# A two-layer hybrid decoder on one core: block 0's gate matmuls after the third input projection, output weights loaded later, the last products on VectorE

## The chip, the cores and the metric

The kernel runs on one core of one Trainium2 chip. The metric is the device time of one execution in microseconds; the time before is the median of three runs, 927.42 us (927.25 to 930.23). The engines are TensorE (PE in the profile), VectorE (DVE), ScalarE (ACT), GpSimd (POOL), and SyncE (SP), which here issues nearly all DMAs.

## What is computed

Input x is 1024 x 1024 in float32. Layer 0 mixes tokens by latent attention with 12 heads, layer 1 by a gated linear recurrence over 12 x 64 channels; both also attend with 4 heads to 256 memory tokens. In each layer:

```python
z = h @ w_in                                   # mixer inputs | gate | memory queries
tok = causal_attention(...) or rg_lru_branch(u, ...)
mem_out = memory_attention(q_mem, mem_k, mem_v)
y = concatenate([tok, mem_out], -1) * silu(gate)
h = layer_norm(ALPHA * h + y @ w_out[layer], ln_g[layer], ln_b[layer])
# the recurrence of layer 1:
xc = conv_b + sum(u_pad[:, tap:tap + s] * conv_w[tap] for tap in range(4))
r, i = sigmoid(xc @ w_r + b_r), sigmoid(xc @ w_i + b_i)      # per block of 64
a = exp(-8 * softplus(-lam) * r)
hs = scan(a, sqrt(1 - a * a) * (i * xc))
```

## The kernel before

Every product is made of three matmuls (`mm3`, lines 110 to 115): each operand is split into a high half in fp32r and a low half, the rest; hi*hi, hi*lo and lo*hi are added up in PSUM. `split` (86 to 90) makes the halves: ACT, DVE or POOL copies the high one (line 82 on POOL, 84 on ACT), and DVE always subtracts to get the low one (line 90). `load_w` (99) brings a weight into one of two staging tiles `wf` and splits it into a ring of two hi/lo tiles; a staging tile is free for the next load when its split is done.

The Tile framework builds one list of instructions per engine from the program's order and its own estimates; an engine runs its list in order and waits at a row until its semaphores are there.

*Layer 0.* `main_head` gives the attention of a head as units: scores, two exponentials (558, 559), a subtraction for the low half of the probabilities (561, mostly POOL), and the products with the values (569). `run_units` (592) runs a head pair's 28 units, and between them takes steps of the generators in `fills`: `n` steps over the units. For the last pair, p = 5 (line 812), the fill is the memory's load, keys and values, the row maxima of two memory heads, and four steps of `wgen`, which loads and splits the eight 128-row pieces of the output weights (`load_wout`, 775). Then the memory attention runs in two pairs of heads (817 to 823), whose fills take one, one and two steps of `wgen`; line 825 takes whatever steps are left.

When the second head of a pair is through, `finish_pair` (621) divides by the softmax sums: two DMAs bring the sums `den` to `rn`, DVE inverts them (625), two DMAs write them to `den_d`, two more broadcast them into `Of` (630), and POOL multiplies (631). Slots 0 to 5 are the head pairs of layer 0, slots 6 and 7 its two memory pairs, slots 8 and 9 those of layer 1. Slot 7's product is on `GA[3]`, printed GA_75.

The output projection `out_proj` (831) starts with a group of three row tiles s = 0, 1, 2: first the feature pieces k = 0 to 3 of all three, then k = 4 to 7. `ymm0` (923) loads the rows of y from `y_d` into `Pf` (929) and splits them into R16 and R17 in turn (printed R_70 and R_71; lines 84 and 934); piece 7 comes from GA[3] itself.

*Layer 1.* Six blocks of 128 channels: `lru_u` is the input projection (48 matmuls), `lru_copy` (995) copies it out of PSUM by ACT, `lru_conv` (999) is the convolution, one instruction of line 1002 and three of 1005 on DVE, with a split, and `lru_rest` (1009) holds the 12 gate matmuls with XH and XL, the activations and the scan. The two first projections come ahead of the list. The string `ORD` (1062) sets the program order of all the rest: c copy, v convolution, r gates and scan, u projection, q memory query projection, g gate projections of the memory part. U, XC, XH, XL, RR and II have two buffers each, one for even and one for odd blocks. Behind it, `pd` opens over the freed buffers and loads the keys, values and queries of the memory attention (1089 on).

Of the kernel before, what the change touches and what calls it, by code (L numbers as in the profile page):

```python
# [15 lines left out]
ALU = mybir.AluOpType  # L16
# [28 lines left out]
def hybrid_kernel(ctx: ExitStack, tc: tile.TileContext, io):  # L45
    nc = tc.nc
    PE, ACT, DVE, POOL, SP = nc.tensor, nc.scalar, nc.vector, nc.gpsimd, nc.sync
# [25 lines left out]
    R = [pr[1].tile([128, S], F32R, name=f"R{i}") for i in range(12)]  # L73
# [3 lines left out]
    def f32(ap):  # L77
        return ap.bitcast(F32)
# [18 lines left out]
    def wsplit(src, hi, lo):  # L97
        split(src, hi, lo, weng[0])

    def load_w(ap, n):  # L100
        j = wjob[0]
        wjob[0] += 1
        st = wf[j % 2][:, :n]
        SP.dma_start(st, ap)
        nb = len(ring["hi"])
        hi, lo = ring["hi"][j % nb], ring["lo"][j % nb]
        wsplit(st, hi[:, :n], lo[:, :n])
        return hi, lo

    def mm3(out, parts):  # L110
        n = len(parts)
        for i, (lh, ll, rh, rl) in enumerate(parts):
            PE.matmul(out, lh, rh, start=(i == 0), stop=False)  # L113
            PE.matmul(out, lh, rl, start=False, stop=False)  # L114
            PE.matmul(out, ll, rh, start=False, stop=(i == n - 1))  # L115
# [59 lines left out]
    with tc.manual_schedule(engines={mybir.EngineType.DVE}):  # L175
# [20 lines left out]
        for k in range(3, 8):  # L196
# [4 lines left out]
                       fill=1.0, base=0, channel_multiplier=1)  # L201
    POOL.memset(cmask, 0.0)
    POOL.affine_select(out=cmask[:, 384:512], in_=cmask[:, 384:512], pattern=[[-1, 128]], compare_op=ALU.is_ge,
                       fill=-1e30, base=0, channel_multiplier=1)
    POOL.memset(cmaskT, 0.0)
    POOL.affine_select(out=cmaskT, in_=cmaskT, pattern=[[1, 128]], compare_op=ALU.is_ge,
                       fill=-1e30, base=0, channel_multiplier=-1)
# [183 lines left out]
    def rope_rows(h):  # L391
        r0 = (h % 4) * 32
        SP.dma_start(f32(sets[h % 4][2])[64:96, :], qr_d[h // 4, 0, r0:r0 + 32, :])
        SP.dma_start(f32(sets[h % 4][3])[64:96, :], qr_d[h // 4, 1, r0:r0 + 32, :])
# [15 lines left out]
    def next_m():  # L410
        mi[0] += 1
        return mbank[mi[0] % len(mbank)]
# [11 lines left out]
    def neg_max_row(mx, dst_row):  # L424
        nm = small.tile([128, 8], F32, tag="nm", name="nm")
        DVE.tensor_reduce(out=nm, in_=mx, axis=AX.X, op=ALU.max, negate=True)

        def row():
            ps = next_m()
            PE.transpose(ps[0:8, 0:128], nm, ident)  # L430
            nmt = small.tile([8, 128], F32R, tag="nmt", name="nmt", bufs=1)
            DVE.tensor_copy(nmt, ps[0:8, 0:128])
            SP.dma_start(f32(dst_row()).rearrange("o (a b) -> o a b", a=8), f32(nmt))
        rows.append([DELAY, row])
# [31 lines left out]
    r1 = slice(32, 64)  # L466
# [119 lines left out]
    def chain(*gens):  # L586
        for g in gens:
            yield from g
# [32 lines left out]
    def finish_pair(gt, slot):  # L621
        rn = small.tile([128, 16], F32, tag="rn", name="rn")
        for e in range(2):
            SP.dma_start(rn[:, e * 8:(e + 1) * 8], den[32 * e:32 * e + 1, :].rearrange("o (a b) -> o a b", a=128))
        DVE.reciprocal(rn, rn)
        for e in range(2):
            SP.dma_start(den_d[slot, e].rearrange("(a b) -> a b", a=128), rn[:, e * 8:(e + 1) * 8])
        rec = Of[slot % 2]
        for e in range(2):
            SP.dma_start(rec[e * 64:(e + 1) * 64, :], den_d[slot, e:e + 1, :].broadcast_to([64, S]))  # L630
        POOL.tensor_tensor(out=gt, in0=gt, in1=rec, op=ALU.mult)

    SC = 1.0 / math.sqrt(96.0)

# [48 lines left out]
    def mem_load():  # L683
        for i in range(2):
            j = wjob[0]
            wjob[0] += 1
            SP.dma_start(wf[j % 2], io["memT"][i])
            wsplit(wf[j % 2], R[i], R[2 + i])
        yield

    def mem_kv(layer):
        KH, KL = (R[4], R[5]) if layer == 0 else (R[8], R[9])
        VmH, VmL = (R[6], R[7]) if layer == 0 else (R[0], R[1])
        pk = next_m()
        for m in range(2):
            hi, lo = load_w(io["wmk"][layer, m], S)
            out = pk[:, m * 256:(m + 1) * 256]
            mm3(out, [(hi[:, k * 128:(k + 1) * 128], lo[:, k * 128:(k + 1) * 128], mTh[k], mTl[k]) for k in range(8)])
            yield
        for e in range(2):  # L700
            src = pk[e * 64:(e + 1) * 64, 0:512].rearrange("p (m k) -> p m k", m=2)
            oh = KH[0:64, :].rearrange("p (m e k) -> p m e k", m=2, e=2)[:, :, e, :]
            ol = KL[0:64, :].rearrange("p (m e k) -> p m e k", m=2, e=2)[:, :, e, :]
            o2 = KH[64:128, :].rearrange("p (m e k) -> p m e k", m=2, e=2)[:, :, e, :]
            ACT.copy(oh, src)
            ACT.copy(o2, src)
            DVE.tensor_tensor(out=ol, in0=src, in1=f32(oh), op=ALU.subtract)
        POOL.memset(f32(KL)[64:65, :], 1.0)
        wv = [load_w(io["wmv"][layer, i], S) for i in range(2)]
        pv_ = next_m()  # L710
        for kt in range(2):
            parts = []
            for k in range(8):
                hi, lo = wv[k // 4]
                c = slice((k % 4) * 256, (k % 4 + 1) * 256)
                parts.append((mTh[k][:, kt * 128:(kt + 1) * 128], mTl[k][:, kt * 128:(kt + 1) * 128], hi[:, c], lo[:, c]))
            mm3(pv_[:, kt * 256:(kt + 1) * 256], parts)
            yield
        src = pv_.rearrange("p (t h d) -> p t h d", t=2, h=4)
        oh = VmH[:, 0:520].rearrange("p (t h d) -> p t h d", t=2, h=4)  # L720
        ol = VmL[:, 0:520].rearrange("p (t h d) -> p t h d", t=2, h=4)
        ACT.copy(oh[:, :, :, 0:64], src)
        DVE.tensor_tensor(out=ol[:, :, :, 0:64], in0=src, in1=f32(oh)[:, :, :, 0:64], op=ALU.subtract)
        POOL.memset(f32(oh)[:, :, :, 64:65], 1.0)
        POOL.memset(f32(ol)[:, :, :, 64:65], 0.0)
        if layer == 1:
            SP.dma_start(mem_d[0], f32(KH))
            SP.dma_start(mem_d[1, 0:65], f32(KL)[0:65, :])
            SP.dma_start(mem_d[2, :, 0:520], f32(VmH)[:, 0:520])
            SP.dma_start(mem_d[3, :, 0:520], f32(VmL)[:, 0:520])  # L730

    def mem_max(layer, m, q1, q2, KH):
        r0 = (m % 2) * 64
        SP.dma_start(f32(q1)[0:64, :], qmem_d[layer][m // 2, 0, r0:r0 + 64, :])
        SP.dma_start(f32(q1)[64:128, :], qmem_d[layer][m // 2, 1, r0:r0 + 64, :])
        SP.dma_start(f32(q2)[0:64, :], qmem_d[layer][m // 2, 0, r0:r0 + 64, :])
        mx = small.tile([128, 8, 2], F32, tag="mx", name="mx")
        POOL.memset(mx, -3.0e38)
        for i4 in range(4):
            ps = next_m()  # L740
            for i2 in range(2):
                i = i4 * 2 + i2
                PE.matmul(ps[:, i2 * 256:(i2 + 1) * 256],
                          q1[:, i * 128:(i + 1) * 128], KH[:, m * 256:(m + 1) * 256], start=True, stop=True)
            DVE.tensor_reduce(out=mx[:, i4 * 2:i4 * 2 + 2, 0:1], in_=ps.rearrange("p (a b) -> p a b", a=2),
                              axis=AX.X, op=ALU.max)
            yield
        neg_max_row(mx, lambda: q2[64:65, :])
        yield
# [36 lines left out]
    MQ = [sets[m][2:4] for m in range(4)]  # L786
# [4 lines left out]
    wgen = load_wout(0, wt, woh, wol)  # L791

    def take(g, n):
        for _ in range(n):
            next(g, None)
            yield

    for p in range(6):
        units = main_head(2 * p) + main_head(2 * p + 1)
        fill, n = [], 0  # L800
        if p < 5:
            rope_rows(2 * p + 2)
            rope_rows(2 * p + 3)
            fill.append(qk_proj(p + 1))
            n += 4
            if p % 2 == 1:
                fill.append(v_proj((p + 1) // 2))
                n += 4
            fill += [max_pass(2 * p + 2), max_pass(2 * p + 3)]
            n += 28  # L810
        else:
            fill += [mem_load(), mem_kv(0), mem_max(0, 0, *MQ[0], R[4]), mem_max(0, 1, *MQ[1], R[4]), take(wgen, 4)]
            n = 19
        fills = [(chain(*fill), n, 0, len(units))]
        run_units(units, fills)
    mbank[:] = [bank[6], bank[7]]
    for q in range(2):
        units = mem0(2 * q) + mem0(2 * q + 1)
        if q == 0:
            fill, n = chain(mem_max(0, 2, *MQ[2], R[4]), take(wgen, 1), mem_max(0, 3, *MQ[3], R[4]), take(wgen, 1)), 12  # L820
        else:
            fill, n = chain(mem_kv(1), take(wgen, 2)), 6
# [236 lines left out]
                DVE.tensor_tensor(out=G1[m][:, cs], in0=ps[n], in1=G1[m][:, cs], op=ALU.mult)  # L1059
            yield  # L1060

    ORD = 'c0 v0 c1 v1 r0 u2 c2 v2 r1 u3 c3 v3 r2 u4 c4 v4 r3 u5 c5 v5 r4 q0 r5 q1 g6 g7'
    for it in ORD.split():
        t = int(it[1])
        if it[0] == 'c':
# [135 lines left out]
```

## Time and profile before

| | |
|---|---|
| median of 3 runs | 927.42 us (927.25 to 930.23) |
| profiled execution | 928.3 us, span 926.5 us |
| mean granted clock of TensorE | 0.993 of full |
| busy: PE, DVE, ACT, POOL | 897.6, 607.4, 438.1, 224.6 us |
| DMA | 96.09 MB, mean 104 GB/s |

The span is the time between the first and the last instruction that the profile shows; 1.8 us of the execution lie around it. Busy times of the engines overlap. An idle time in brackets stands in front of an instruction and names what ended it. Of TensorE's clock, 1.00 is 2.4 GHz and 0.50 is 1.2 GHz.

### The profile page before, as it was taken

The page shows a single profiled execution, that of the slowest core. Times are in us where ns is not written, and L with a number is a line of the kernel's source. Part 1 is how long each engine was busy: PE and PEld are TensorE (multiplying, and loading weights), DVE is VectorE, ACT ScalarE, POOL GpSimd, SP SyncE. Part 2 cuts the span into 40 slices and gives each one's busy share as a digit, 9 for nine tenths or more (in the row PEclk, how much of TensorE's full clock was granted, in tenths as well). Part 3 has the DMA queues.
Part 4 walks back from the last instruction along what each step waited for, and adds up shares of the span by engine and source line. Part 5 has one row for each costly group of instructions (what it writes and reads, how often), then busy time and mean ns, then how long its engine had stood idle before and what let it go on. Part 6 is the DMA issues. An engine that isn't in the chain of part 4 may idle for free.

```text
span 926.5 us, 12547 instructions
## 1 busy us (share of the span) xinstructions
PE 897.6 (97%) x4477; PEld 733.6 (79%) x4477; DVE 607.4 (66%) x1309; ACT 438.1 (47%) x747; POOL 224.6 (24%) x219
## 2 busy tenths in 40 slices
PE   9999999999999999999999999988999999999996
PEld 8998788877787778779677878866888877678886
DVE  7953256258777768795784498746998154457865
ACT  4423211217676677777785122117997156753000
POOL 5101033011536354473771200000000022210000
PEclk9999999999999999999999999998999999999999
DMA  9102134324022213155657552111112911252311
GB/s 329 44 23 100 54 111 147 96 76 106 15 58 69 59 58 104 33 160 142 196 144 230 175 180 102 68 69 46 46 46 104 242 54 47 69 181 93 137 72 65
DMA packets 45658, 96.09 MB, mean 104 GB/s; under 512 B 10874, under 2 KB 19866, under 8 KB 45596
## 3 DMA queue, kind: packets, MB, share of 16 engines
q1 hardware_dynamic: 45164, 94.60, 32.6%
q8 instruction: 35, 0.57, 0.3%
q10 hardware_dynamic: 432, 0.69, 0.2%
q14 instruction: 27, 0.22, 0.1%
HBM read 71.94 MB, written 23.16 MB: 103 GB/s over the span
## 4 chain that ended last, share of the span: by engine, by line
PE 79%; DVE 7%; ACT 4%; issue 3%; DMA 3%; POOL 2%; SPq 0%; DVEq 0%; ACTq 0%; POOLq 0%
PE bank L113 10%; PE bank L114 10%; PE bank L115 10%; PE bank L569 7%; PE bank L654 5%; PE bank L844 5%; PE bank L843 5%; PE bank L842 5%; PE bank L364 3%; PE bank L366 3%; PE bank L365 3%; PE bank L154 2%; PE bank L155 2%; PE bank L153 2%; PE bank L451 2%
## 5 line engine op out<-in xcount | busy, mean ns | idle before, releaser
L561 POOL TENSOR_TENSOR pl<-Pf,ph 128x512 fp32r<-128x512 f32 (+1 forms) x99 | 125.4, 1277 | 116.5 <-ACT ph L559 102.8
L558 ACT ACTIVATE Pf<-bank 128x512 f32<-128x512 f32 (+1 forms) x152 | 86.5, 569 | 52.6 <-DVE bank L555 20.8
L654 PE MATMUL bank<-st,st 96*128 96x512 f32 (+7 forms) x432 | 106.0, 344 | 0.1
L90 DVE TENSOR_TENSOR R<-wf,R 128x1024 fp32r<-128x1024 f32 (+4 forms) x43 | 52.1, 1214 | 64.2 <-POOL R L82 60.1
L654 PEld LDWEIGHTS bank<-st,st 96*128 96x128 f32 (+1 forms) x432 | 76.0, 190 | 13.3 <-ACT ph L559 0.6
L559 ACT ACTIVATE ph<-bank 128x512 fp32r<-128x512 f32 (+1 forms) x136 | 76.4, 563 | 0.1
L82 POOL TENSOR_SCALAR R<-wf 128x1024 fp32r<-128x1024 f32 (+3 forms) x25 | 24.1, 966 | 197.1 <-PE bank L114 95.6
L113 PE MATMUL bank<-R,R 128*128 128x256 f32 (+1 forms) x190 | 63.2, 333 | 0.7 <-ACT Pf L372 0.4
L114 PE MATMUL bank<-R,R 128*128 128x256 f32 (+1 forms) x190 | 62.3, 328 | 0.0
L115 PE MATMUL bank<-R,R 128*128 128x256 f32 (+1 forms) x190 | 62.2, 327 | 0.0
L453 DVE CUSTOM_DVE_ANT_0 bank<-bank,cmask 128x384 f32<-128x384 f32 (+4 forms) x96 | 48.8, 518 | 10.7 <-PE bank L451 9.8
L364 PE MATMUL bank<-xh,R 128*128 128x512 f32 x128 | 50.8, 397 | 0.1
L366 PE MATMUL bank<-xh,R 128*128 128x512 f32 x128 | 50.7, 396 | 0.0
L365 PE MATMUL bank<-xl,R 128*128 128x512 f32 x128 | 50.5, 395 | 0.0
L569 PE MATMUL bank<-ph,VH 128*65 128x512 f32 (+2 forms) x144 | 49.5, 344 | 0.0
L569 PE MATMUL bank<-pl,VH 128*65 128x512 f32 (+2 forms) x144 | 45.3, 341 | 2.4 <-POOL pl L561 2.0
L569 PE MATMUL bank<-ph,VL 128*65 128x512 f32 (+2 forms) x144 | 47.1, 338 | 0.0
L843 PE MATMUL bank<-wo,yh 128*128 128x512 f32 (+1 forms) x126 | 47.0, 373 | 0.0
L842 PE MATMUL bank<-wo,yh 128*128 128x512 f32 (+1 forms) x126 | 46.6, 370 | 0.0
L844 PE MATMUL bank<-wo,yl 128*128 128x512 f32 (+1 forms) x126 | 45.9, 368 | 0.0
L114 PE MATMUL bank<-HTl,rg 128*128 128x512 f32 x112 | 44.4, 396 | 0.0
L113 PE MATMUL bank<-HTh,rg 128*128 128x512 f32 x112 | 44.3, 396 | 0.0
(314 smaller groups left out, 2390.5 us busy)
## 6 DMA issues: line engine op xcount, KB each, us to landing
wf<-w SPq DMA_DIRECT2D x26, 512.0 KB, 3.6
wf<-wout SPq DMA_DIRECT2D x16, 512.0 KB, 3.9
Of<-den_d SPq DMA_DIRECT2D x20, 256.0 KB, 3.6
GA<-x SPq DMA_DIRECT2D x8, 512.0 KB
h_d<-GA SPq DMA_DIRECT2D x8, 512.0 KB, 2.6
GA<-h_d SPq DMA_DIRECT2D x8, 512.0 KB, 4.1
y_d<-GA SPq DMA_DIRECT2D x7, 512.0 KB
out<-GA SPq DMA_DIRECT2D x7, 512.0 KB
```

Source lines behind the costliest of these rows:

```text
L113: PE.matmul(out, lh, rh, start=(i == 0), stop=False)
L114: PE.matmul(out, lh, rl, start=False, stop=False)
L115: PE.matmul(out, ll, rh, start=False, stop=(i == n - 1))
L364: PE.matmul(ps[n], hi[:, ks], xh[k][:, cs], start=(k == 0), stop=False)
L366: PE.matmul(ps[n], lo[:, ks], xh[k][:, cs], start=False, stop=(k == 7))
L558: ACT.activation(pf[:, :n], ps[:, :n], AF.Exp, scale=scale)
L561: lo_eng.tensor_tensor(out=lo[:, :n], in0=pf[:, :n], in1=f32(hi)[:, :n], op=ALU.subtract)
L569: mm.append(lambda: PE.matmul(ops[0:65, q0:q0 + w], st, mv[:, c0:c0 + w], start=start, stop=stop))
L654: yield lambda: PE.matmul(ps[:, c0:c0 + w], k[0:r, ks], q[0:r, qs], start=(i == 0), stop=(i == 2))
L842: PE.matmul(out, hi, woh[k][:, ns], start=(k == ko[0]), stop=False)
L843: PE.matmul(out, hi, wol[k][:, ns], start=False, stop=False)
L844: PE.matmul(out, lo, woh[k][:, ns], start=False, stop=(k == ko[7]))
```

## The change

Three edits. `finish_pair` multiplies on DVE instead of POOL for slots 7, 8 and 9. The fill of the last head pair loses its four steps of `wgen`, and n goes from 19 to 15; the later takes of one, one and two and line 825 stay as they are. `ORD` is written anew: each block's gates r follow the projection of two blocks later, which itself moves ahead of the next convolution; r4 and r5 follow q0 and q1.

```diff
@@ -628,7 +628,8 @@
-        POOL.tensor_tensor(out=gt, in0=gt, in1=rec, op=ALU.mult)
+        eng = DVE if slot >= 7 else POOL
+        eng.tensor_tensor(out=gt, in0=gt, in1=rec, op=ALU.mult)
@@ -809,8 +810,8 @@
-            fill += [mem_load(), mem_kv(0), mem_max(0, 0, *MQ[0], R[4]), mem_max(0, 1, *MQ[1], R[4]), take(wgen, 4)]
-            n = 19
+            fill += [mem_load(), mem_kv(0), mem_max(0, 0, *MQ[0], R[4]), mem_max(0, 1, *MQ[1], R[4])]
+            n = 15
@@ -1059,7 +1060,7 @@
-    ORD = 'c0 v0 c1 v1 r0 u2 c2 v2 r1 u3 c3 v3 r2 u4 c4 v4 r3 u5 c5 v5 r4 q0 r5 q1 g6 g7'
+    ORD = 'c0 v0 c1 u2 v1 r0 c2 v2 u3 c3 r1 v3 u4 c4 r2 v4 u5 c5 r3 v5 q0 r4 q1 r5 g6 g7'
```

From line 632 on, a line of the changed kernel has a number higher by one. How the lists of the engines change is shown at two places.

VectorE at the first convolutions of layer 1, before. XC_5437, XH_5439 and XL_5441 belong to block 0, XC_5438 and XL_5442 to block 1; R_71 is the low half of the third projection's weights, rg_5431 that of the fourth's:

```order
L1002 TENSOR_SCALAR XC_5437<-U_5435,vecs 128x1024
L1002 TENSOR_SCALAR XC_5438<-U_5436,vecs 128x1024
L1005 SCALAR_TENSOR_TENSOR XC_5437<-U_5435,vecs,XC_5437 128x1024
L1005 SCALAR_TENSOR_TENSOR XC_5438<-U_5436,vecs,XC_5438 128x1024
L1005 SCALAR_TENSOR_TENSOR XC_5437<-U_5435,vecs,XC_5437 128x1024
L1005 SCALAR_TENSOR_TENSOR XC_5438<-U_5436,vecs,XC_5438 128x1024
L1005 SCALAR_TENSOR_TENSOR XC_5437<-U_5435,vecs,XC_5437 128x1024
L1005 SCALAR_TENSOR_TENSOR XC_5438<-U_5436,vecs,XC_5438 128x1024
L90 TENSOR_TENSOR XL_5441<-XC_5437,XH_5439 128x1024
L90 TENSOR_TENSOR R_71<-wf_82,R_70 128x1024
```

and of the change:

```order
L1003 TENSOR_SCALAR XC_5437<-U_5435,vecs 128x1024
L1003 TENSOR_SCALAR XC_5438<-U_5436,vecs 128x1024
L1006 SCALAR_TENSOR_TENSOR XC_5437<-U_5435,vecs,XC_5437 128x1024
L1006 SCALAR_TENSOR_TENSOR XC_5438<-U_5436,vecs,XC_5438 128x1024
L1006 SCALAR_TENSOR_TENSOR XC_5437<-U_5435,vecs,XC_5437 128x1024
L90 TENSOR_TENSOR R_71<-wf_82,R_70 128x1024
L1006 SCALAR_TENSOR_TENSOR XC_5437<-U_5435,vecs,XC_5437 128x1024
L1006 SCALAR_TENSOR_TENSOR XC_5438<-U_5436,vecs,XC_5438 128x1024
L90 TENSOR_TENSOR XL_5441<-XC_5437,XH_5439 128x1024
```

R_71 moved up, ahead of three convolution steps; the second row, the first step of block 1, stands where it stood. On TensorE the 12 gate matmuls of block 0 moved from ahead of the third projection's first product with R_71 to behind the projection's last.

VectorE at the start of layer 0's output projection, before. R_70<-Pf_76, R_71<-Pf_77 and R_70<-Pf_78 are the low halves of y for row tiles 0, 1 and 2, pieces 0 to 3:

```order
L618 TENSOR_TENSOR GA_75<-bank_87,GA_75 64x512
L561 TENSOR_TENSOR pl_114<-Pf_79,ph_110 128x512
L934 TENSOR_TENSOR R_70<-Pf_76,R_70 128x512
L618 TENSOR_TENSOR GA_75<-bank_88,GA_75 64x512
L934 TENSOR_TENSOR R_71<-Pf_77,R_71 128x512
L625 RECIPROCAL rn<-rn 128x16
L934 TENSOR_TENSOR R_70<-Pf_78,R_70 128x512
```

and of the change:

```order
L935 TENSOR_TENSOR R_70<-Pf_76,R_70 128x512
L618 TENSOR_TENSOR GA_75<-bank_87,GA_75 64x512
L561 TENSOR_TENSOR pl_114<-Pf_79,ph_110 128x512
L90 TENSOR_TENSOR st_1_1782<-wf_82,st_0_1781 128x1024
L618 TENSOR_TENSOR GA_75<-bank_88,GA_75 64x512
L90 TENSOR_TENSOR st_1_1786<-wf_83,st_0_1785 128x1024
L625 RECIPROCAL rn<-rn 128x16
L90 TENSOR_TENSOR VL_1794<-wf_82,VH_1791 128x1024
L90 TENSOR_TENSOR st_3_1547<-wf_83,st_2_1546 128x1024
L632 TENSOR_TENSOR GA_75<-GA_75,Of_81 128x1024
L935 TENSOR_TENSOR R_71<-Pf_77,R_71 128x512
L935 TENSOR_TENSOR R_70<-Pf_78,R_70 128x512
```

The low halves of four pieces of the output weights (four rows of line 90) and slot 7's product (line 632) came in ahead of the second row tile's low half.

The queue of SP there, of the change:

```order
L771 DMA y_d<-GA_74 128x1024
L624 DMA rn<-den 128x1x8
L781 DMA wf_82<-wout 128x1024
L834 DMA Of_80<-ln_g 128x1024
L627 DMA den_d<-rn 128x8 x2
L781 DMA wf_83<-wout 128x1024
L630 DMA Of_81<-den_d 64x1024 x2
L930 DMA Pf_77<-y_d 128x4x128
```

The load of Pf_77 stood ahead of the first of these rows before, and stands behind slot 7's broadcast into Of_81 now.

## Rows read from the trace of the kernel before

**Rows 1.** The page: span and instructions, busy time and share of PE and others.

```profile
span 926.5 us, 12547 instructions
...
PE 897.6 (97%) x4477; PEld 733.6 (79%) x4477; DVE 607.4 (66%) x1309; ACT 438.1 (47%) x747; POOL 224.6 (24%) x219
```

**Rows 2.** Timeline of PE, layer 1: start, length, instruction, count, idle time before.

```profile
621.96 0.40 PE L114 MATMUL bank<-HTl,rg 128*128 128x512 f32 x1
629.21 2.07 PE L113 MATMUL bank<-XH,WGH 128*128 128x512 f32 x4 [6.86 <-ACT XH L84]
...
634.13 0.40 PE L115 MATMUL bank<-HTh,R 128*128 128x512 f32 x1
```

**Rows 3.** Timeline of DVE in the same place.

```profile
621.24 0.81 DVE L1002 TENSOR_SCALAR XC<-U,vecs 128x1024 f32<-128x1024 f32 x1 [7.31 <-ACT U L997]
621.96 7.26 DVE L1005 SCALAR_TENSOR_TENSOR XC<-U,vecs,XC 128x1024 f32<-128x1024 f32 x6
...
630.33 1.22 DVE L90 TENSOR_TENSOR R<-wf,R 128x1024 fp32r<-128x1024 f32 x1
```

**Rows 4.** Windows: stretch, length, busy PE, PEld, DVE, ACT, POOL; clock, DMA.

```profile
632.00:633.00 1.00, 1.00 (x4) 0.81 (x3) 1.00 (x2) 0.69 (x1) 0.00 (x0) 0.50 0.36 66
231.00:232.00 1.00, 1.00 (x5) 0.81 (x4) 1.00 (x3) 0.38 (x1) 0.48 (x1) 0.50 0.00 0
```

**Rows 5.** Timeline of PE: the longest wait of the memory attention, layer 0.

```profile
487.66 0.50 PE L762 MATMUL bank<-st,R 128*128 128x512 f32 x1 [1.40 <-ACT ph L559]
```

**Rows 6.** Timeline of POOL, DVE and PE around slot 8's product.

```profile
803.23 2.38 POOL L631 TENSOR_TENSOR GB<-GB,Of 128x1024 f32<-128x1024 f32 x1 [7.21 <-DMA Of<-den_d]
...
803.75 3.00 DVE L561 TENSOR_TENSOR mpl<-Pf,mph 128x512 fp32r<-128x512 f32 x2 [1.79 <-ACT mph L559]
...
806.20 0.45 PE L569 MATMUL bank<-mpl,VH 128*65 128x512 f32 x1 [1.59 <-DVE mpl L561]
```

**Rows 7.** Timeline: SP's first load, and PE's first score, of layer 1's memory attention.

```profile
718.71 0.37 SPq L1089 DMA_DIRECT2D KH<-mem_d  x1
...
741.29 0.88 PE L743 MATMUL bank<-KH,mq 128*128 128x256 f32 x6
```

**Rows 8.** The page: subtractions of line 90, and loads of output weights.

```profile
L90 DVE TENSOR_TENSOR R<-wf,R 128x1024 fp32r<-128x1024 f32 (+4 forms) x43 | 52.1, 1214 | 64.2 <-POOL R L82 60.1
...
wf<-wout SPq DMA_DIRECT2D x16, 512.0 KB, 3.9
```

**Rows 9.** Windows over the memory attention and the start of the output projection.

```profile
500.00:520.00 20.00, 20.00 (x87) 16.14 (x87) 4.65 (x10) 3.25 (x7) 4.47 (x2) 1.00 0.69 201
440.00:460.00 20.00, 18.76 (x105) 14.06 (x102) 16.27 (x27) 15.33 (x29) 16.05 (x12) 1.00 0.69 200
460.00:480.00 20.00, 19.15 (x113) 15.36 (x114) 15.04 (x27) 17.88 (x34) 14.26 (x12) 1.00 0.53 144
480.00:500.00 20.00, 18.13 (x105) 13.52 (x104) 14.84 (x19) 15.24 (x26) 6.89 (x7) 1.00 0.68 218
```

**Rows 10.** Timeline of PE: the first matmul of layer 0's output projection.

```profile
498.99 0.49 PE L842 MATMUL bank<-st,R 128*128 128x512 f32 x1
```

**Rows 11.** Timeline of DVE: low half of row tile 1.

```profile
502.07 0.69 DVE L934 TENSOR_TENSOR R<-Pf,R 128x512 fp32r<-128x512 f32 x1 [1.53 <-ACT R L84]
```

**Rows 12.** Timeline of SP's queue: y of row tile 1, then slot 7's transfers.

```profile
497.90 0.58 SPq L929 DMA_DIRECT2D Pf<-y_d  x1
...
502.53 0.50 SPq L624 DMA_DIRECT2D rn<-den  x1
...
505.57 0.80 SPq L627 DMA_DIRECT2D den_d<-rn  x2
...
508.49 1.12 SPq L630 DMA_DIRECT2D Of<-den_d  x2
```

**Rows 13.** Timeline of POOL: slot 7's product.

```profile
515.04 2.39 POOL L631 TENSOR_TENSOR GA<-GA,Of 128x1024 f32<-128x1024 f32 x1 [12.96 <-DMA Of<-den_d]
```

**Rows 14.** Line 631 by itself: duration ns min/median/max, first and last start.

```profile
L631 POOL TENSOR_TENSOR GA<-GA,Of x8: 2392/2400/3375, 277.2 to 515.0; 128x1024 f32<-128x1024 f32 x8
```

## The prediction

> **What bounds the kernel now.** The page comes first: TensorE (PE) is busy for 897.6 of 926.5 us [rows 1], so only what keeps it waiting, or slows its clock, can move the time; the 28.9 us in which it is not busy are all there is to win, and every new wait is lost in full. Next the timeline of PE, read for the idle time in brackets. The longest wait is in layer 1: after the early part of the third input projection PE stops from 622.36 to 629.21, 6.86 us, for XH, the converted result of the first convolution [rows 2]. The timeline of VectorE (DVE) tells why [rows 3]: it had idled for 7.31 us in front of the second block's first convolution instruction, which waits for a copy of the second projection, although the first block's next instruction stood right behind it. So DVE takes its list strictly in order, and whatever waits at its head holds all that follows. After the stall the granted clock is 0.50, the lower level of 1.2 GHz [rows 4]: the 12 gate matmuls take 629.21 to 634.13 = 4.92 us instead of 12 x 0.23 = 2.76. That adds 2.16 us to the stall.
>
> **Part 1, the order of layer 1's blocks.** The gate matmuls of block 0 (12) move behind the third projection (48 matmuls, 11.2 us). But that projection waits as well: its third product needs the low half of its weights, R_71, and in the new order DVE makes it after the second block's first instruction and three of the six further convolution steps. From 621.96, with 7.26/6 = 1.21 us each [rows 3], that is 621.96 + 4 x 1.21 = 626.8. Before, the corresponding matmul started at 634.13 [rows 2], with the 12 gate matmuls and two early ones of the fourth projection already done; these 14 now come later (2.76 + 0.47 us). Gain: 634.13 - 626.8 - 3.2 = 4.1 us at full clock. PE still stops for 626.8 - 621.9 = 4.9 us. For the clock behind that the nearest rows differ: a wait of 6.86 us was followed by 0.50, and a shorter one, near 228 us, too [rows 4]; waits of 1.40 and 1.59 us were not [rows 5, 6]; the matmuls behind them have the usual 0.23 us from start to start. 4.9 is nearest to 6.86, so I take the same loss of 2.1. Part 1 gains **2.0**; between 4.1 (clock stays) and 0 (the low clock lasts twice as long).
>
> The last block's gates now come after both memory query projections. The loads for layer 1's memory attention reuse that block's buffers and now stand behind one weight load more. Before, they were issued 741.29 - 718.71 = 22.6 us ahead of use [rows 7]; now the extra load waits for a projection (11.2 us) more, but part of that wait was there anyway, so about 11 to 14 us remain. Weight loads of the same size land in 3.9 us in the median [rows 8], and only the first few transfers are needed at once. I take 0; should the cover go, the price is the few us by which they miss.
>
> **Part 2, the output weights of layer 0.** Four of the eight pieces no longer load beside head pair 5. The later steps still take one, one and two, so four pieces do load during the memory attention, and the other four now fall behind it, into the start of the output projection. What the removal may win are the waits between 440 and 500: 60 - (18.76 + 19.15 + 18.13) = 3.96 us [rows 9]. The largest, 1.40 us [rows 5], stands ahead of 24 matmuls of the memory values; in the new order that score matmul comes behind them, so they cover it. Of the other 2.56 I take a quarter, because the conversions moved off here stay on the same two engines. Gain **2.0**, between 0 and 4.0.
>
> **Part 3, the products on DVE.** For slots 8 and 9 (layer 1): while POOL ran slot 8's product from 803.23, DVE's subtraction beside it ended only at about 806.2, and PE waited 1.59 us [rows 6]. With the product on DVE the first subtraction is done in 0.69, but the next stands behind a product of 1.21 us (the two-input form of line 90, [rows 8]), so about half of the wait stays: gain **0.8**, between 0 and 1.6. Slot 9's product comes when its factors have landed and nothing near it is urgent: 0.
>
> Slot 7 (layer 0) is where this meets part 2. PE starts the output projection at 498.99 [rows 10]; the first half of the first row tile is 24 matmuls and one is left over from the attention, 25 x 0.23 = 5.8, so it is through at 504.8. Before, the second tile's low half was made at 502.07 [rows 11], and 500 to 520 shows no wait [rows 9]. Now that row (R_71<-Pf_77) stands on DVE behind the four late pieces and behind slot 7's product. The product waits for Of<-den_d: the sums go out at 502.53, their inverses at 505.57, the broadcast at 508.49 [rows 12], and POOL could start its product only at 515.04, after 12.96 us of waiting [rows 13]. None of these steps is shortened, for they begin with the last attention unit. The load of Pf_77, issued at 497.90 before, now stands behind the broadcast as well (about 509.6; 3.5 us later it is in, as 497.90 to 501.4 before), so not even the high half is there before 513.7. The last weight piece, issued behind the inverses at about 506.4, is in at 510.3 by 3.9 us a load [rows 8] and ahead of the broadcast.
>
> So: product 515.04 + 1.21 = 516.25; subtraction 0.69 [rows 11] = 516.9. PE waits from 504.8 to 516.9 = 12.1 us; two matmuls that need only high halves fit in before (0.47): **11.6 lost**, between 9.5 and 14 if the chain of transfers ends 2 us sooner or later. Clock behind it: 2.1 as behind the stall of [rows 2], between 0 and 4.2. Nothing later gives this back: PE goes on without slack.
>
> Here a rule speaks the other way. POOL's product takes 2400 ns [rows 14], DVE's two-input instructions 1214 [rows 8]. The Trainium skill (GPSIMD Engine Reference, Engine selection) says to put elementwise work on VectorE, GpSimd being about twice as slow with two inputs; the trace agrees on that ratio. By it the sum for slot 7 would be a gain of 2.40 - 1.21 = 1.2 us. By the order on DVE it is a loss of 11.6, since what counts is who stands behind a waiting product: behind it on POOL stood nothing that PE needed.
>
> **Sum.** 11.6 + 2.1 - 2.0 - 2.0 - 0.8 = +8.9 us. The profiled execution took 928.3 (span 926.5 and 1.8 around it): 937.2. It lies 0.9 above the median of the runs, 927.4, so the forecast for the median is **936.3**.
>
> **Rivals.**
> - *The product does not hold PE up* (faster). Mechanism: the broadcast lands before PE runs dry. It decides at about 502.9: product and subtraction then end at 504.8. The gains of the parts would stand alone: 927.4 - 2.0 - 2.0 - 0.8 = 922.6, and with their upper ends 927.4 - 4.0 - 4.1 - 1.6 = 917.7. The engine rule above, taken alone, would add its 1.2. For it: the engine ratio, and the waits of [rows 9]. Against: 515.04 in [rows 13], twelve us too late, in a chain that starts when the attention ends. Chance 0.08.
> - *Loss and gain cancel* (no change): stall at its low end 9.5, no low clock, gains near their upper ends (9.7): 927.2, and up to 930.2. Chance 0.10.
> - *The late weights are the later ones*: each of the four pieces waits for the buffer of the one two before; if they take 6 us a load rather than 3.9 beside the other traffic, the last is converted only after the broadcast, and the wait grows by 2 to 4 us, with the low clock longer: 940 to 945. Chance 0.12.
> - *The change does not do what its words say*: "during the memory attention" holds for four pieces of eight, and the gates of block 0 lose one wait to another. Both are in the forecast.
>
> **How the numbers follow.** The forecast, with its own range of 931 to 940, gets 0.70. Of faster or slower I speak from 0.3%, 2.8 us, about what a measurement of this kernel can tell from no change. Faster (under 924.6): 0.08. Same: 0.10. Slower (over 930.2): 0.70 + 0.12 = 0.82. The range leaves out the faster case, most of the cancelling one and the far end of the late one: 929.5 to 943.
>
> **What would show it.** Right: a PE wait of 10 us or more early in layer 0's output projection, ended by line 935 or by the cast ahead of it; DVE idle before line 632 until Of has landed; a PE wait near 5 us before the third projection's third product, and none of 6.9 before the gates; a granted clock of 0.50 behind both; about half of the wait near 806 left. Wrong: no wait over 3 us in the output projection, or line 632 on GA starting within 4 us of its start; a third projection that runs through; a new wait at the first memory scores of layer 1.

## The result and the profile after

The changed kernel takes 937.96 us in the median of four runs (936.37 to 941.63), against 927.34 for the kernel before (four runs by now): ratio 1.0118, 95% interval 1.0092 to 1.0143. It is slower by 10.6 us; 936.3 was forecast, in a range of 929.5 to 943.

The profiled execution is the slowest of the four, 941.6 us with a span of 939.8, so the two profiles lie 13.3 us apart and the medians 10.6. Part of the excess arises where nothing was changed: a matmul that starts at 207.84 in the profile before starts at 209.60 in this one. Times below are therefore differences inside one profile, or medians. The page, span and PE's share, answering to [rows 1]:

```profile
span 939.8 us, 12547 instructions
...
PE 903.2 (96%) x4477; PEld 740.1 (79%) x4477; DVE 611.0 (65%) x1312; ACT 441.6 (47%) x748; POOL 216.0 (23%) x216
```

PE is not busy for 36.6 us where it was 28.9. Its waits, grouped by the line that waited and what ended the wait (total, times, longest, in us):

```profile
PE bank L843 <- ACT R L84: 11.3, 1, 11.3
PE bank L115 <- DVE R L90: 4.9, 1, 4.9
PE bank L569 <- POOL pl L561: 3.7, 3, 2.1
```

The first did not exist before. The second takes the place of the 6.86 us of [rows 2]. On PE's timeline the first lies in the output projection of layer 0, between the first row tile (s = 0) and the second:

```profile
503.30 0.39 PE L843 MATMUL bank<-st,R 128*128 128x512 f32 x1
...
508.88 0.40 PE L845 MATMUL bank<-VH,R 128*128 128x512 f32 x1
520.59 0.79 PE L843 MATMUL bank<-st,R 128*128 128x512 f32 x1 [11.32 <-ACT R L84]
521.18 0.63 PE L844 MATMUL bank<-st,R 128*128 128x512 f32 x1
```

What the cast waited for stands on SP's queue, answering to [rows 12]. The load of y for the second row tile is the first of four on the last line; before, it went out ahead of the first line here:

```profile
507.64 0.50 SPq L624 DMA_DIRECT2D rn<-den  x1
...
510.71 0.80 SPq L627 DMA_DIRECT2D den_d<-rn  x2
511.61 0.38 SPq L781 DMA_DIRECT2D wf<-wout  x1
513.96 1.12 SPq L630 DMA_DIRECT2D Of<-den_d  x2
515.13 2.21 SPq L930 DMA_DIRECT2D Pf<-y_d  x4
```

ACT's cast of it, and VectorE (DVE) with the low half of the last late piece of the weights, slot 7's product, and the low half of the row tile:

```profile
519.92 0.62 ACT L84 CAST R<-Pf 128x512 fp32r<-128x512 f32 x1 [3.71 <-DMA Pf<-y_d]
```

```profile
516.25 1.23 DVE L90 TENSOR_TENSOR st<-wf,st 128x1024 fp32r<-128x1024 f32 x1 [1.47 <-ACT st L84]
519.35 1.23 DVE L632 TENSOR_TENSOR GA<-GA,Of 128x1024 f32<-128x1024 f32 x1 [1.88 <-DMA Of<-den_d]
520.57 0.69 DVE L935 TENSOR_TENSOR R<-Pf,R 128x512 fp32r<-128x512 f32 x1
```

Two things end within 0.1 us of each other here: the cast, 519.92 + 0.62 = 520.54, and the product, 519.35 + 1.23 = 520.58. PE's wait ended with the cast, for the first two matmuls of the tile need only the high half; but the low half, which the third needs, was made behind the product. So the profile alone does not say what either would have cost without the other. The granted clock, by stretches, behind the waits of 2.1, 11.3 and 4.9 us (the third number from the end of a row; 0.50 is the lower level):

```profile
454.00:457.00 3.00, 3.00 (x17) 2.91 (x16) 1.15 (x4) 0.97 (x2) 2.40 (x3) 0.55 1.01 259
521.00:525.00 4.00, 4.00 (x10) 3.02 (x10) 0.96 (x2) 0.46 (x1) 0.00 (x0) 0.50 0.95 293
644.00:648.00 4.00, 4.00 (x11) 3.12 (x10) 4.00 (x4) 1.04 (x1) 0.00 (x0) 0.50 0.39 131
```

Behind 11.32 us, 12 matmuls take 520.59 to 525.88 = 5.29 instead of 2.8 us: 2.5 lost. In layer 1, answering to [rows 2, 3]:

```profile
643.38 0.79 PE L115 MATMUL bank<-HTh,R 128*128 128x512 f32 x1 [4.93 <-DVE R L90]
```

```profile
637.79 0.81 DVE L1003 TENSOR_SCALAR XC<-U,vecs 128x1024 f32<-128x1024 f32 x1 [7.32 <-ACT U L998]
638.52 3.67 DVE L1006 SCALAR_TENSOR_TENSOR XC<-U,vecs,XC 128x1024 f32<-128x1024 f32 x3
642.11 1.22 DVE L90 TENSOR_TENSOR R<-wf,R 128x1024 fp32r<-128x1024 f32 x1
```

DVE idles 7.32 us in front of the second block's row, as before, and the low half that PE now waits for is the fifth row from there. Near 822, where [rows 6] had a wait of 1.59 us, PE has none.

### The profile page after: what moved, and what is told of

Same layout as the page of the kernel before. It is cut to its first block, busy times and chain, and to the rows that moved or that the text cites. A ratio compares the mean times of both kernels' runs of the same rounds, so it can differ in the third digit from the quotient of the medians.

```text
span 939.8 us, 12547 instructions
## 1 busy us (share of the span) xinstructions
PE 903.2 (96%) x4477; PEld 740.1 (79%) x4477; DVE 611.0 (65%) x1312; ACT 441.6 (47%) x748; POOL 216.0 (23%) x216
## 4 chain that ended last, share of the span: by engine, by line
PE 83%; DVE 6%; ACT 5%; issue 3%; DMA 3%; POOL 1%; SPq 0%; DVEq 0%; ACTq 0%; POOLq 0%
PE bank L113 10%; PE bank L115 10%; PE bank L114 10%; PE bank L569 7%; PE bank L843 6%; PE bank L844 6%; PE bank L845 6%; PE bank L655 5%; PE bank L364 3%; PE bank L365 3%; PE bank L366 3%; PE bank L154 2%; PE bank L155 2%; PE bank L153 2%; PE bank L451 2%
## 5 line engine op out<-in xcount | busy, mean ns | idle before, releaser
L561 POOL TENSOR_TENSOR pl<-Pf,ph 128x512 fp32r<-128x512 f32 (+1 forms) x99 | 121.0, 1230 | 124.6 <-ACT ph L559 100.4
L115 PE MATMUL bank<-HTh,R 128*128 128x512 f32 x112 | 45.4, 406 | 4.9 <-DVE R L90 4.9
L114 PE MATMUL bank<-HTl,R 128*128 128x512 f32 x112 | 45.2, 404 | 0.0
```

Of the source, the lines that this page charges most:

```text
L561: lo_eng.tensor_tensor(out=lo[:, :n], in0=pf[:, :n], in1=f32(hi)[:, :n], op=ALU.subtract)
```

## The experiments

The edits (a) product, (b) fill and (c) order were first run apart and taken back one by one. Times are medians; each ratio is to the kernel before on the same chip (928.0, 927.7 and 927.3 us in the three batches).

| run | us | ratio, 95% interval |
|---|---|---|
| fill_alone | 941.51 | 1.0148, 1.0124 to 1.0172 |
| slot7_on_pool | 937.65 | 1.0105, 1.0084 to 1.0127 |
| fill_restored | 924.57 | 0.9962, 0.9939 to 0.9985 |
| y_on_pool_queue | 929.05 | 1.0010, 0.9991 to 1.0028 |
| order_alone | 926.42 | 0.9984, 0.9968 to 1.0000 |
| products_alone | 925.31 | 0.9968, 0.9951 to 0.9986 |
| u2_low_on_pool | 917.66 | 0.9886, 0.9863 to 0.9910 |
| slot6_on_dve | 916.49 | 0.9880, 0.9858 to 0.9902 |
| eight_in_memory_attention | 935.40 | 1.0090, 1.0056 to 1.0123 |

**fill_alone**, from the kernel before:

```diff
-            fill += [mem_load(), mem_kv(0), mem_max(0, 0, *MQ[0], R[4]), mem_max(0, 1, *MQ[1], R[4]), take(wgen, 4)]
-            n = 19
+            fill += [mem_load(), mem_kv(0), mem_max(0, 0, *MQ[0], R[4]), mem_max(0, 1, *MQ[1], R[4])]
+            n = 15
```

> The kernel before with only the four steps of wgen taken out of the last head pair's fill; all products stay on POOL. Theory A (the product on VectorE holds TensorE up): no wait over 3 us in layer 0's output projection, 925 to 928 us. Theory B (the fill alone does it: the load of the second row tile of y falls behind the broadcast of slot 7's sums on SP): a wait of 10 to 11.5 us there, ended by the cast or the low half of that tile, half the clock for about 5 us behind it; 927.3 + 11 + 2.4 + about 1 for the memory attention = 939 to 943 us.

Theory B held: 13.5 us slower with every product on POOL. PE's timeline, the wait in the memory attention and the one in the output projection:

```profile
448.48 0.63 PE L569 MATMUL bank<-pl,VH 128*65 128x512 f32 x1 [2.11 <-POOL pl L561]
...
515.73 0.79 PE L842 MATMUL bank<-st,R 128*128 128x512 f32 x1 [11.52 <-ACT R L84]
```

The second has the same cause on SP's queue as in the changed kernel, the load of y behind the broadcast:

```profile
508.41 1.12 SPq L630 DMA_DIRECT2D Of<-den_d  x2
509.57 2.33 SPq L929 DMA_DIRECT2D Pf<-y_d  x4
```

The first bears on the gain expected of part 2. On POOL's timeline slot 5's product stands directly ahead of three subtractions of probabilities, for the first of which PE waits:

```profile
444.33 2.39 POOL L631 TENSOR_TENSOR GA<-GA,Of 128x1024 f32<-128x1024 f32 x1
...
446.75 4.58 POOL L561 TENSOR_TENSOR pl<-Pf,ph 128x512 fp32r<-128x512 f32 x3
```

Before, it stood directly ahead of two in the same way, but ran 2.5 us earlier, and PE waited 0.64 us:

```profile
441.86 2.40 POOL L631 TENSOR_TENSOR GA<-GA,Of 128x1024 f32<-128x1024 f32 x1
444.23 3.52 POOL L561 TENSOR_TENSOR pl<-Pf,ph 128x512 fp32r<-128x512 f32 x2
```

```profile
445.56 0.45 PE L569 MATMUL bank<-pl,VH 128*65 128x512 f32 x1 [0.64 <-POOL pl L561]
```

By stretches of fill_alone, answering to [rows 9]:

```profile
440.00:460.00 20.00, 17.08 (x90) 13.65 (x89) 12.90 (x23) 14.96 (x28) 13.40 (x12) 0.91 0.59 173
460.00:480.00 20.00, 20.00 (x122) 16.52 (x121) 13.38 (x27) 16.13 (x31) 11.25 (x13) 1.00 0.27 68
480.00:500.00 20.00, 19.15 (x111) 14.58 (x111) 14.02 (x20) 16.46 (x27) 8.95 (x7) 1.00 0.72 223
```

From 460 to 500 PE idles 0.85 us where it idled 2.72 before; from 440 to 460 it idles 2.92 where it was 1.24.

**slot7_on_pool**, from the changed kernel:

```diff
-        eng = DVE if slot >= 7 else POOL
+        eng = DVE if slot >= 8 else POOL
```

> The changed kernel with slot 7's product back on POOL (slots 8 and 9 stay on VectorE). Theory A: the wait in the output projection goes, 938.0 - 13.7 = 924 us. Theory B: the tile's load still lands at about 519.9 behind the broadcast, so the wait is 10.5 to 11.3 us and the time 937 to 938 us.

Theory B again: 937.65 us, 0.3 from the changed kernel, and with no product on DVE's list PE still waits:

```profile
516.42 0.80 PE L843 MATMUL bank<-st,R 128*128 128x512 f32 x1 [11.00 <-ACT R L84]
```

**fill_restored**, from the changed kernel, puts the two lines of the fill back as they were before.

> The changed kernel with the four steps of wgen back in the last head pair (n = 19). Slot 7's product stays on VectorE. Theory A: the product is behind the broadcast as ever, and a wait of 8 us or more remains; 933 us or more. Theory B: no wait over 1.5 us in the output projection; the gains of the order of layer 1's blocks (1.4) and of slot 8's product (1.5) stand alone: 927.3 - 2.9 = 924.4 us.

The long wait is gone while slot 7's product stays on DVE, and the time, 924.57 us, is that of theory B. The longest wait in the output projection is now one in the first row tile, a little over the 1.5 us that theory B allowed (more on it with what was unexpected); it stands in a profiled run of 929.2 us, and the other runs need not have it:

```profile
504.73 0.50 PE L845 MATMUL bank<-st,R 128*128 128x512 f32 x1 [1.88 <-DVE R L935]
```

**y_on_pool_queue**, from slot7_on_pool:

```diff
-        SP.dma_start(t[:, 0:nk], y_d[kh * 4:kh * 4 + nk, :, sl].rearrange("k p t -> p k t"))
+        (POOL if i in (1, 2) else SP).dma_start(t[:, 0:nk], y_d[kh * 4:kh * 4 + nk, :, sl].rearrange("k p t -> p k t"))
```

> The changed kernel with slot 7's product on POOL, and the loads of y for the second and third row tile issued by POOL instead of SP; the late weights stay late. If it is the place in SP's queue that counts (theory B), the second row tile is there before TensorE needs it, and no wait over 2 us is left at its first matmul: 938.0 - 13.7 + 1 = 924 to 926 us. If it is the late weight pieces themselves (their transfers or their splits), a wait of 5 to 11 us stays in the first three row tiles: 931 to 938 us.

The wait at the second row tile is gone, and 8.6 us with it, although four weight pieces are as late as ever. The first matmul of that tile:

```profile
513.36 0.40 PE L843 MATMUL bank<-st,R 128*128 128x512 f32 x1
```

The time is 3 to 5 us above what theory B gave, because the lists were laid out anew: the cast of that tile moved ahead of the last exponentials on ACT and waits 6.75 us for its load there, which POOL had issued at 491.74, and PE waits for an exponential behind it:

```profile
499.26 0.62 ACT L84 CAST R<-Pf 128x512 fp32r<-128x512 f32 x1 [6.75 <-DMA Pf<-y_d]
```

```profile
501.40 1.12 PE L569 MATMUL bank<-ph,R 128*65 128x512 f32 x2 [4.33 <-ACT ph L559]
```

**eight_in_memory_attention**, from slot7_on_pool:

```diff
-            fill, n = chain(mem_max(0, 2, *MQ[2], R[4]), take(wgen, 1), mem_max(0, 3, *MQ[3], R[4]), take(wgen, 1)), 12
+            fill, n = chain(mem_max(0, 2, *MQ[2], R[4]), take(wgen, 2), mem_max(0, 3, *MQ[3], R[4]), take(wgen, 2)), 14
-            fill, n = chain(mem_kv(1), take(wgen, 2)), 6
+            fill, n = chain(mem_kv(1), take(wgen, 4)), 8
```

> slot7_on_pool with the takes of the memory attention raised from one, one and two to two, two and four (n from 12 to 14 and from 6 to 8), so that all eight pieces of the output weights load there and none behind it. On SP's list the loads of y for the first two row tiles now stand behind the sums of slot 7, which go out when the last unit is through. Theory (a load waits for whatever stands ahead of it on SP): the first row tile's load is issued about 503 and in at about 507, TensorE has run dry at about 500.5: a wait of 6 to 8 us with half the clock behind it; 927.8 - 1.3 - 1.6 + 7 + 2 = 934 us, 932 to 937. Rival (only pieces that load after the attention cost time): no wait over 2 us there, 924 to 926 us.

The theory held, in size too: no piece is loaded behind the attention any more (the last load goes out at 502.52), and the first row tile waits instead, because its load stands behind slot 7's sums on SP.

```profile
512.28 0.80 PE L843 MATMUL bank<-st,R 128*128 128x512 f32 x1 [7.66 <-ACT R L84]
```

```profile
503.05 3.42 SPq L624 DMA_DIRECT2D rn<-den  x2
506.52 0.58 SPq L834 DMA_DIRECT2D Of<-ln_g  x1
507.20 0.39 SPq L930 DMA_DIRECT2D Pf<-y_d  x1
```

**order_alone**, the kernel before with the changed string:

```diff
-    ORD = 'c0 v0 c1 v1 r0 u2 c2 v2 r1 u3 c3 v3 r2 u4 c4 v4 r3 u5 c5 v5 r4 q0 r5 q1 g6 g7'
+    ORD = 'c0 v0 c1 u2 v1 r0 c2 v2 u3 c3 r1 v3 u4 c4 r2 v4 u5 c5 r3 v5 q0 r4 q1 r5 g6 g7'
```

> The kernel before with the changed ORD alone. Theory (part 1 as in the prediction): the wait of 6.86 us before the gates goes and one of 4.9 us comes before the third product of the third projection, with the half clock behind it as long as before; 928.0 - 2.0 = 926 us. Rival (the blocks' order gains nothing, what fill_restored won came from the products): 927.5 to 928.5 us.

The wait has the size of the theory, and the median falls by 1.3; the interval reaches to 1.0000, so the gain as such is not quite told from none.

```profile
627.10 0.79 PE L115 MATMUL bank<-HTh,R 128*128 128x512 f32 x1 [4.93 <-DVE R L90]
```

**products_alone**, the kernel before with slots 7 to 9 on DVE:

```diff
-        POOL.tensor_tensor(out=gt, in0=gt, in1=rec, op=ALU.mult)
+        eng = DVE if slot >= 7 else POOL
+        eng.tensor_tensor(out=gt, in0=gt, in1=rec, op=ALU.mult)
```

> The kernel before with the products of slots 7, 8 and 9 on VectorE, fill and ORD as before. Theory: the wait of 1.6 us near 806 goes entirely, slot 7 costs nothing because the load of the second row tile and its low half stand ahead of the product; 928.0 - 1.6 = 926.4 us. Rival (the product on VectorE costs at slot 7): 930 us or more.

It is 2.4 us faster. The wait near 806 is gone whole, and slot 7 costs nothing where the second row tile's load and low half stand ahead of its product. DVE with slot 8's product between two subtractions; PE uses the second of them at 805.59 without a wait:

```profile
802.93 0.69 DVE L561 TENSOR_TENSOR mpl<-Pf,mph 128x512 fp32r<-128x512 f32 x1 [1.79 <-ACT mph L559]
803.54 1.22 DVE L632 TENSOR_TENSOR GB<-GB,Of 128x1024 f32<-128x1024 f32 x1
804.68 0.68 DVE L561 TENSOR_TENSOR mpl<-Pf,mph 128x512 fp32r<-128x512 f32 x1
```

**u2_low_on_pool** keeps ORD as changed and the fill as before, has slots 8 and 9 on DVE, and one more edit:

```diff
-        DVE.tensor_tensor(out=lo, in0=src, in1=f32(hi), op=ALU.subtract)
+        leng[0].tensor_tensor(out=lo, in0=src, in1=f32(hi), op=ALU.subtract)
...
     def lru_u(t):
+        leng[0] = POOL if t == 2 else DVE
         hi, lo = load_w(io["w1"][t], S)
+        leng[0] = DVE
```

> fill_restored with slot 7's product on POOL and with the low half of the third projection's weights made by POOL instead of VectorE, so that it doesn't stand behind the second block's convolution. Theory (only the place on VectorE's list makes TensorE wait 4.9 us): POOL has the low half at about 7 us before TensorE asks for it, the wait goes and with it the 2.4 us that half the clock costs: 924.6 - 7.3 = 917.3 us. Rival (the gates then wait for block 0's convolution, which stands behind the same row): a wait of 3 to 5 us before the gates, 920 to 923 us.

The theory held to 0.4 us: 917.66. POOL has the low half at 616.9, 6 us before PE asks for it (622.91), and over 60 us around it PE is busy throughout, at the full clock:

```profile
614.54 2.39 POOL L90 TENSOR_TENSOR R<-wf,R 128x1024 fp32r<-128x1024 f32 x1
```

```profile
600.00:620.00 20.00, 20.00 (x90) 15.81 (x89) 10.88 (x22) 2.74 (x5) 5.01 (x5) 1.00 0.29 106
620.00:640.00 20.00, 20.00 (x88) 16.19 (x87) 13.91 (x12) 9.27 (x12) 2.05 (x1) 1.00 0.16 54
640.00:660.00 20.00, 20.00 (x88) 16.12 (x87) 15.18 (x12) 17.36 (x20) 1.96 (x1) 1.00 0.08 26
```

Order and products together bring 3.4 us without this edit (fill_restored) and 10.0 with it (slot 7's product on POOL); a part of the difference may be the 1.88 us wait of fill_restored's profile, which this one does not have. A wait of 1.21 us for a load of queries shows at layer 1's first memory scores in this profile, and none there in that of slot6_on_dve.

**slot6_on_dve**, from u2_low_on_pool, with `eng = DVE if slot >= 6 and slot != 7 else POOL`.

> u2_low_on_pool with slot 6's product on VectorE too (slot 7 on POOL). In fill_restored's profile a low half on VectorE took 2.87 us instead of 0.69 beside slot 6's product on POOL, and TensorE waited 1.88 us for it with half the clock behind. If the two engines hold each other up there, the wait goes: 1 to 3 us less than u2_low_on_pool. If VectorE's wait for the broadcast delays the second row tile's low half instead: 1 us more or no change.

916.49 us, the fastest of all, 11.2 under the kernel before. Against u2_low_on_pool it stays open: the 1.2 us between them lie inside the two intervals, and in u2_low_on_pool's profile the two engines did not meet, so the wait of 1.88 us had not come up there.

## Why the prediction was right, and which steps were not

The time and the sign were right, the place and the size of the main loss too. The cause that the sum was worked out with is not the one that the runs show.

- **The stall in the output projection.** 11.6 forecast, 11.32 measured; the clock behind it 2.1 forecast, 2.5 measured. The step that failed is "So: product 515.04 + 1.21 = 516.25; subtraction 0.69". It took the product as the last thing to end and treated the load of y, "not even the high half is there before 513.7", as the lesser condition. fill_alone makes 11.52 us without any product on DVE, and taking the product away from the changed kernel leaves 11.00. What holds PE up is the load of the second row tile, which stands behind slot 7's chain on SP once four weight loads are late. Its issue was forecast well (about 509.6; fill_alone has 509.57), its length was not: I had 3.5 us, and as the first of four issued together it takes 4.8 us (515.13 to 519.92), 5.5 in fill_alone and 5.1 in slot7_on_pool. Whether the three behind it make it longer, no run tells. Both chains start from the same sums of slot 7 and pass the same broadcast, which is why a wrong cause gave a right size. Luck had its share: counted from the issue of the broadcast, PE ran dry 1.0 us earlier than forecast and went on 1.3 us earlier. One thing stays open: wherever the load is early (products_alone, fill_restored), the tile's low half stands ahead of the product on DVE's list. No run has the load early and the low half behind the product, so what that place on the list would cost by itself is not shown.
- **The engine rule.** The prediction set a gain of 1.2 us for slot 7, by the ratio of the two engines, against a loss of 11.6, by the order on DVE. With slot 7 on DVE or POOL the changed kernel takes 937.96 or 937.65 us: neither can be seen. The Trainium skill (GPSIMD Engine Reference, Engine selection) puts such work on VectorE, as GpSimd is about twice as slow with two inputs. The ratio holds here (1.23 us on DVE, 2.35 on POOL in slot7_on_pool), but at this place the time does not follow from it.
- **Part 1**, 2.0 forecast: order_alone wins 1.3. The wait came out as 4.93 for a forecast of 4.9. Behind it 12 matmuls take 643.38 to 648.66 = 5.28 us, 2.5 lost for 2.1. The memory loads behind it cost nothing, as forecast: PE has no wait at the first memory scores.
- **Part 2's gain**, 2.0 forecast, came and was lost again. "They cover it" held: the wait of 1.40 us is gone (the 24 matmuls named are 48 of half the width in the trace), and from 460 to 500 PE idles 1.87 us less in fill_alone. The step that failed is "of the other 2.56 I take a quarter", which took away old waits without looking for new ones: from 440 to 460 PE idles 1.68 us more, most of it in the wait of 2.11 us, with the clock at 0.50 behind it. From the wait at 409.05 to the first matmul of the output projection, 498.22, the stretch takes 89.2 us, and before, from 410.43 to 498.99, 88.6.
- **Part 3**, 0.8 forecast: products_alone wins 2.4. "About half of the wait stays" failed: the product takes 1.22 us between two subtractions, and the second was still in time. That accounts for 1.6; the other 0.8 is not explained and is less than the interval.

The parts, measured apart, add up: +13.5 (fill), -1.3 (order), -2.4 (products) = +9.8 against 10.6 for all three. Of the rivals, the late-weight one did not come: the last piece's low half was done at 517.48, before the product began at 519.35, and y_on_pool_queue, with its pieces as late, has no wait at the second row tile. The late pieces cost by where they put the load of y. The faster one needed the broadcast before PE runs dry; PE ran dry at 509.28, and the product began ten us later.

## What to carry to other kernels

A transfer that is moved later is paid for by what then stands behind it in its queue: read the queue's list at the place where it lands, and find the next load there that TensorE needs. When two conditions end a wait at nearly the same time, a forecast of its length says nothing of the cause; undo each alone. And an engine whose list has a waiting row at its head holds up everything behind: moving one needed instruction to an idle engine, though it takes twice as long there, was worth some 7 us.

## What was unexpected of the hardware

A VectorE subtraction of two tiles in SBUF stood still while POOL multiplied two others. In fill_restored, DVE's low half of the first row tile and slot 6's product on POOL:

```profile
501.81 2.87 DVE L935 TENSOR_TENSOR R<-Pf,R 128x512 fp32r<-128x512 f32 x1
```

```profile
501.77 2.37 POOL L632 TENSOR_TENSOR GA<-GA,Of 128x1024 f32<-128x1024 f32 x1 [3.41 <-DMA Of<-den_d]
```

POOL ends at 504.14 and DVE at 504.68, 0.54 later, for an instruction that takes 0.69 alone; PE waited 1.88 us for it. The stretched pair in [rows 6] has the same look, and two more runs repeat it: beside slot 6's product on POOL a subtraction that takes 0.69 us alone took 2.81 in eight_in_memory_attention and 2.67 in y_on_pool_queue, ended 0.55 and 0.56 us after POOL, and PE waited 2.20 and 0.98 us. Where DVE began first, it was POOL's product that took longer, 3.33 us instead of 2.39 (fill_alone, at 498.79). The Trainium skill (SBUF — State Buffer, Who interferes with whom) says that a VectorE instruction with two SBUF inputs and a GpSimd one that reads SBUF exclude each other, and whoever starts first holds the port to its end; these rows agree. So the price of a product on POOL is not its place on POOL alone; that products_alone, without slot 8's there, loses the whole wait near 806 fits this.

And a wait's length did not tell the clock behind it: 2.1 us (fill_alone, 449 to 451) and 1.88 us (fill_restored, 506 to 509) were followed by 0.50, and so was the one of 1.3 us near 230 [rows 4], but 1.40 [rows 5] and 1.59 [rows 6] were not.
